# Eleven weight tiles of a two-layer mixer split into rounded part and remainder by DMAs instead of by ScalarE and VectorE

## The chip, the cores and the metric

One Trainium2 chip, and one of its cores. The metric is the time of one execution of the kernel on the device, in microseconds (us); lower is better. The engines are called PE (TensorE, matmuls), ACT (ScalarE), DVE (VectorE), POOL (GpSimd) and SP (SyncE, which here issues nearly all DMAs).

## The reference

Two layers. Each adds a mixer and then a mixture of experts to the stream `x` (256 tokens of 1024 channels, float32).

```python
h = rms_norm(x, norm_mix_g[l]) * (1.0 + sc_m) + sh_m
x = x + g_m * mixer(h, ...)
h = rms_norm(x, norm_ffn_g[l]) * (1.0 + sc_f) + sh_f
x = x + g_f * moe_ffn(h, ...)
...
proj = h @ w_in                      # in the mixer: 1024 x 7168
qa, ka, va, ub, qc, kc, vc, gates = jnp.split(proj, IN_SPLITS, axis=-1)
y_a = diff_attention(qa, ka, va) @ w_proj_a      # norm and rotary on qa, ka before
y_b = conformer_conv(ub, ...) @ w_proj_b + b_proj_b
y_c = stick_breaking(qc, kc, vc) @ w_proj_c
g = jax.nn.sigmoid(gates)            # three gates of 1024 channels
merged = g[0] * y_a + g[1] * y_b + g[2] * y_c
return merged @ w_out
```

The vectors sc_m, sh_m, g_m and so on come from `c_act @ w_mod[l]`, whose weights are read too ("mod" below). The mixture of experts has 64 experts, of which each token uses 8, and a shared one.

## The kernel before

The kernel runs, in this order: mixer of layer 0 (up to about 330 us of the profile), experts of layer 0 (to about 820), mixer of layer 1 (to about 1135), experts of layer 1 (to the end at 1628.8).

Weights come in tiles of 2 MB (128 partitions x 4096 float32), each by two DMAs of 128x2048 that SP issues (L218). The tiles stand in one list, `st`, in the order in which they are needed. Five slots of this size, `w`, take them in turn, and a load waits until the tile that was in its slot has been used. In the mixer `w_in` is 14 such tiles: qa, ka, va, uba, ubg (the two halves of ub), qc, kc, vc and six gate tiles ga0, ga1, gb0, gb1, gc0, gc1. Each tile makes four output chunks of 128 channels. The mod tiles stand between them and are summed on DVE (L530, 1024 columns at a time).

A chunk is a sum over 1024 channels in eight parts of 128. Most parts are computed in float32r (a shorter float32) with a correction. The activations stand as a rounded `hH` and a remainder `hL`, made once in `mix_norm`. The weights of each half chunk (four parts, 128x512) are split in `split`, L686 and L687:

```python
se.activation(H[:, j:], src, AF.Copy)                              # ACT: WH, rounded
ve.tensor_tensor(Lo[:, j:], src, H[:, j:].bitcast(F32), op=OP.subtract)   # DVE: WL, the remainder
```

Three matmuls then stand for each part, hH by WH, hL by WH, hH by WL (`mmj`). The other parts are computed in one plain float32 matmul of `plain` (called room in the profile) by the tile itself; the table NAT says how many of the eight. For `w_in` that is none in layer 0 and three in layer 1, so that there only the last five parts are split (WH is 128x128 and 128x512 in turn). Five pairs of WH and WL are kept (NSPLIT), made ahead of the matmuls (`ahead`).

PE's order is written by a planner: attention and convolution pieces run as generators between the half chunks (`mm_piece`), at a rate set by constants. The convolution is 31 steps on DVE for each of four channel groups (L765, room<-room,tcol,room, 128x256). The order on ACT, DVE and POOL is the scheduler's, which goes by priority and by what is ready. POOL issues none of the weight loads of the mixers.

In layer 0, after the gate tiles of C, PE comes to the tail of the attention A (lines 927 to 973): the head norms need a reciprocal root that DVE works out in eleven small steps (L455 to L464, 128x8), and PE then transposes its result (L973), before the first projection. In layer 1 the first tiles are qa (chunks up to 842 us) and va.

Of the kernel before, what the change touches and what calls it, by code (L numbers as in the profile page):

```python
# [12 lines left out]
F32R = mybir.dt.float32r  # L13
# [3 lines left out]
OP = mybir.AluOpType  # L17
# [60 lines left out]
NAT = ({"i": 0, "g": 0, "a": 4, "b": 0, "c": 4, "o": 1}, {"i": 3, "g": 3, "a": 4, "b": 0, "c": 0, "o": 3})  # L78
RAW = (1, 5)
# [89 lines left out]
def trunk(ctx, tc, A, out, dbg=None):  # L169
# [51 lines left out]

    def load_halves(src):
        t = []

        def f(k):
            if not k:
                t.append(wtile())
            sp.dma_start(t[0][:, k * 2048:(k + 1) * 2048], src[:, k * 2048:(k + 1) * 2048])
            return t[0]
        return lambda: f(0), lambda: f(1)  # L230
# [39 lines left out]
    for l in range(L):  # L270
# [9 lines left out]
        for k, s in enumerate(seq):  # L280
            if (l or k > 1) and NAT[l][{"in": "g" if s[1] in GATES else "i", "proj": s[1], "out": "o"}[s[0]]] > (4 * s[1] if s[0] == "out" else 0):
                st.held.add(len(st.items))
            if s[0] == "in" and (l or k > 1):
                st.add(("in", l, s[1]), load_tile(A["w_in"][l, s[2] // 512]))
            if s[0] == "proj":
                st.add(("proj", l, s[1]), load_tile(A["w_proj_" + s[1]][l]))
            if s[0] == "out":
                st.add(("out", l, s[1]), load_tile(A["w_out"][l, s[1]]))
            mod_at[l, s[0], s[1]] = here = [mods.pop(0) for _ in range(MOD_AT[l].count(k))]
            for m in here:  # L290
                st.add(("mod",) + m, load_mod(*m))
# [259 lines left out]

    def mix_norm(pool, l):
        i, g = NAT[l]["i"], NAT[l]["g"]
        n = min(i, g)
# [9 lines left out]
        X, XG = parts(i), parts(g)  # L564

# [30 lines left out]
    def mixer_body(l, pool, before=None):  # L596
# [27 lines left out]

        def pieces(o):
            n = plain(*o[0:2])
            return [o + (hf,) for hf in range(2) if n < (4 if o[0] == "proj" else 4 * hf + 4)]
# [13 lines left out]
        order += [p for o in seq for p in pieces(o)]  # L641
        oidx = {o: k for k, o in enumerate(order)}
        got, cur, done = {}, {}, [0]

# [4 lines left out]
        def wget(key):  # L649
            if key not in cur:  # L650
                while not loaded(key):
                    mods.extend(held)
                    held[:] = []
                    assert next(fills_[0])
                cur[key] = st.get((key[0], l, key[1]))
# [56 lines left out]
        def mm_piece(o, key, X, first, last):  # L712
            wn = weights(key) if first_split(key) else None
# [1216 lines left out]
```

## Time and profile before

| | |
|---|---|
| median of 3 runs | 1626.22 us (1619.97 to 1626.4) |
| the profiled execution's own time | 1630.43 us |
| its span in the trace | 1628.8 us |
| PE, DVE, ACT busy | 96%, 46%, 29% of the span |
| ACT L686 and DVE L687, the splits | 272 each; 147.8 and 157.2 us |
| DMA moved | 543.95 MB |

All stretches and moments below are in us from the start of the span of the profiled execution, which took 4.2 us longer than the median of the runs. A busy share of the whole span mixes four stages with different limits, so the rows further down are read by stage.

### The profile page before, as it was taken

The numbers are of one execution on the slowest core, as the hardware profiler recorded it, in microseconds if no ns is written. First come the engines' busy times: TensorE is split into PE (matmuls) and PEld (weight loads), VectorE is DVE, ScalarE is ACT, GpSimd is POOL, SyncE is SP. The second block draws the span as 40 slices with busy tenths as digits, with TensorE's granted clock in tenths as the row PEclk, the third lists the DMA queues.
The fourth block names the chain that finished last, engine by engine and source line by source line (L and its number), as shares of the span: only waits on it lengthen the run. The fifth ranks groups of instructions, "written<-read, shape, count | busy, mean of one in ns | idle before, by whom it ended". The sixth has DMA issues, their size and how long they took to land.

```text
span 1628.8 us, 25000 instructions
## 1 busy us (share of the span) xinstructions
PE 1557.7 (96%) x9710; PEld 1048.9 (64%) x9710; DVE 751.4 (46%) x1866; ACT 468.5 (29%) x911; POOL 2.9 (0%) x26
## 2 busy tenths in 40 slices
PE   6999999999999999899989999999999999998997
PEld 4999869975455454355479888798655455543543
DVE  8799989652222222122249998554422222211122
ACT  3546833421111111111144355244211111111111
POOL 0000000000000000000000000000000000000000
PEclk8999979999999999999989999899999999999999
DMA  9885418959999999999958753256599999999997
GB/s 378 354 326 225 156 53 335 387 211 384 385 419 421 419 418 419 421 420 418 417 238 335 278 214 113 99 218 272 206 381 397 421 419 419 418 419 422 419 418 283
DMA packets 76154, 543.95 MB, mean 334 GB/s; under 512 B 8576, under 2 KB 9216, under 8 KB 12544
## 3 DMA queue, kind: packets, MB, share of 16 engines
q1 hardware_dynamic: 76032, 542.31, 82.1%
q8 instruction: 78, 1.28, 0.3%
q14 instruction: 44, 0.36, 0.1%
HBM read 541.23 MB, written 1.05 MB: 333 GB/s over the span
## 4 chain that ended last, share of the span: by engine, by line
PE 71%; DMA 22%; DVE 4%; ACT 1%; issue 1%; SPq 0%; DVEq 0%; ACTq 0%
PE psA L198 32%; PE psT L198 19%; DMA w<-in_w_dram 15%; PE psS L198 12%; PE psG L198 7%; DMA wx<-in_w_dram 5%; DMA w<-in_w_mod_dram 1%; DVE w L530 1%; DVE WL L687 1%; PE psT L1675 1%; DMA xT<-in_xT_dram 0%; DVE room L765 0%; ACT h L585 0%; DMA w<-in_w_in_dram 0%; DVE nt L584 0%
## 5 line engine op out<-in xcount | busy, mean ns | idle before, releaser
L198 PE MATMUL psT<-w,xe 128*64 128x512 f32 (+2 forms) x1152 | 245.2, 606 | 6.5 <-DMA w<-in_w_dram 6.5
L198 PE MATMUL psT<-wx,xe 128*64 128x512 f32 (+2 forms) x896 | 206.9, 619 | 10.5 <-DMA wx<-in_w_dram 10.4
L198 PE MATMUL psA<-hH,WH 128*128 128x256 f32 x696 | 210.5, 302 | 1.2 <-ACT WH L686 1.2
L1659 DVE TENSOR_SCALAR oT<-psG,slot 128x256 fp32r<-128x256 f32 x54 | 26.1, 484 | 402.0 <-PE psG L198 402.0
L686 ACT ACTIVATE WH<-w 128x512 fp32r<-128x512 f32 (+2 forms) x272 | 147.8, 553 | 204.6 <-PE psA L198 184.9
L1711 DVE SCALAR_TENSOR_TENSOR Y<-psS,gt,Y 128x512 fp32r<-128x512 f32 x108 | 81.1, 751 | 264.1 <-ACT Y L1710 264.1
L198 PE MATMUL psA<-hH,WL 128*128 128x256 f32 x696 | 197.8, 284 | 1.3 <-DVE WL L687 1.3
L198 PE MATMUL psA<-hL,WH 128*128 128x256 f32 x696 | 197.5, 284 | 0.7 <-DVE hL L575 0.7
L687 DVE TENSOR_TENSOR WL<-w,WH 128x512 fp32r<-128x512 f32 (+2 forms) x272 | 157.2, 590 | 59.7 <-ACT WH L686 59.1
L198 PEld LDWEIGHTS psT<-w,xe 128*64 128x64 f32 (+2 forms) x1152 | 77.5, 130 | 140.1 <-issue 122.9
L198 PE MATMUL psA<-room,w 128*128 128x256 f32 x592 | 147.0, 393 | 1.1 <-ACT room L578 1.1
L198 PEld LDWEIGHTS psT<-wx,xe 128*64 128x64 f32 (+2 forms) x896 | 66.5, 132 | 125.4 <-issue 102.6
L1710 ACT ACTIVATE Y<-psS,gt 128x512 fp32r<-128x512 f32 x108 | 74.3, 688 | 219.3 <-PE psS L198 219.3
L198 PEld LDWEIGHTS psA<-hH,WH 128*128 128x128 f32 x696 | 133.1, 191 | 5.1 <-ACT WH L686 2.8
L198 PEld LDWEIGHTS psA<-hL,WH 128*128 128x128 f32 x696 | 133.1, 191 | 3.0 <-DVE hL L575 0.9
L198 PEld LDWEIGHTS psA<-hH,WL 128*128 128x128 f32 x696 | 132.9, 191 | 2.2 <-DVE WL L687 2.1
L1649 ACT ACTIVATE sl<-psT 128x256 f32<-128x256 f32 x54 | 20.7, 383 | 382.8 <-PE psT L198 382.8
L198 PEld LDWEIGHTS psA<-room,w 128*128 128x128 f32 x592 | 110.8, 196 | 17.8 <-issue 2.9
L198 PE MATMUL psA<-oT,Y 128*128 128x256 f32 x864 | 116.0, 286 | 0.9 <-ACT Y L1710 0.8
L530 DVE SCALAR_TENSOR_TENSOR w<-w,room 128x1024 f32<-128x1024 f32 x96 | 115.6, 1219 | 1.1 <-DMA w<-in_w_mod_dram 1.0
L198 PEld LDWEIGHTS psA<-oT,Y 128*128 128x128 f32 x864 | 105.7, 189 | 3.7 <-ACT Y L1710 3.4
L765 DVE SCALAR_TENSOR_TENSOR room<-room,tcol,room 128x256 f32<-128x256 f32 x240 | 103.9, 480 | 0.0
(586 smaller groups left out, 2102.3 us busy)
## 6 DMA issues: line engine op xcount, KB each, us to landing
w<-in_w_dram SPq DMA_DIRECT2D x200, 1024.0 KB, 19.8
wx<-in_w_dram SPq DMA_DIRECT2D x160, 1024.0 KB, 19.3
w<-in_w_in_dram SPq DMA_DIRECT2D x56, 1024.0 KB, 8.2
w<-in_w_mod_dram SPq DMA_DIRECT2D x48, 1024.0 KB, 9.1
w<-in_w_out_dram SPq DMA_DIRECT2D x8, 1024.0 KB, 8.0
wx<-in_w_dram SPq DMA_DIRECT2D x4, 2048.0 KB, 21.6
w<-in_w_dram SPq DMA_DIRECT2D x4, 2048.0 KB, 23.5
w<-in_w_proj_a_dram SPq DMA_DIRECT2D x4, 1024.0 KB, 8.0
```

The lines of the kernel that those rows point to most:

```text
L198: pe.matmul(out=o, lhsT=lhsT, rhs=rhs, start=start, stop=stop, skip_group_check=True)
L530: ve.scalar_tensor_tensor(t[:, j], t[:, j], 1.0, crow, op0=OP.mult, op1=OP.mult, accum_out=modv[l][:, c:c + 1])
L686: se.activation(H[:, j:], src, AF.Copy)
L687: ve.tensor_tensor(Lo[:, j:], src, H[:, j:].bitcast(F32), op=OP.subtract)
L765: ve.scalar_tensor_tensor(yv[:, ch], hp[:, ch, w:w + S], wc, yv[:, ch], op0=OP.mult, op1=OP.add)
L1649: se.activation(sl, b[:, 0:FF], AF.Silu)
L1659: ve.tensor_scalar(oT, bg[:, 0:S], slot[:, k_:k_ + 1], None, op0=OP.is_equal)
L1675: pe.transpose(out=b[:, j * P:(j + 1) * P], in_=hh[:, j], identity=ident)
L1710: se.activation(Y[:, hf], b, AF.Copy, scale=gt)
L1711: ve.scalar_tensor_tensor(Y[:, 2 + hf], b, gt, Y[:, hf].bitcast(F32), op0=OP.mult, op1=OP.subtract)
```

## The change

For the tiles named in CAST (five in layer 0, six in layer 1) the split is made by the DMA queue. `load_cast` loads the tile by two GpSimd DMAs of 128x2048 into a float32r view of a `w` slot: that is the rounded part. A second `w` slot ("lo") is filled in `load_rest`: ACT writes the negated rounded part, and a GpSimd DMA that adds brings the same weights from memory a second time, so that the remainder is left. Each such tile so takes two of the five slots and is read twice. `prepare_upto` starts the second part LEAD = 14 half chunks before the tile is used. The matmuls of these tiles read the slots themselves; there is no WH or WL. In layer 1 all eight parts of `h` are now split (`full`), since the cast tiles use three float32r matmuls for every part; the other tiles still use three plain parts. Counts over the program: splits 272 to 184 on ACT and on DVE each, 22 new negations on ACT, 44 DMAs on POOL, 22 fewer on SP, plain float32 matmuls 72 fewer and 216 float32r ones more, in layer 1 three more `hH` and three more `hL`.

```diff
@@ -76,6 +76,9 @@
        "uba": OFF_UB, "ubg": OFF_UB + 512}
 GATES = [f"g{b}{h}" for b in "abc" for h in range(2)]
 NAT = ({"i": 0, "g": 0, "a": 4, "b": 0, "c": 4, "o": 1}, {"i": 3, "g": 3, "a": 4, "b": 0, "c": 0, "o": 3})
+
+CAST = (("kc", "vc", "ga1", "gc1", "gb1"), ("va", "ubg", "kc", "ga1", "gb1", "gc1"))
+LEAD = 14
 RAW = (1, 5)
 NORM1 = 3
 NORM2 = 5
@@ -218,6 +221,20 @@
                 sp.dma_start(t[:, k * h:(k + 1) * h], src[:, k * h:(k + 1) * h])
             return t
         return f
+
+    def load_cast(src):
+        def f():
+            t = wtile()
+            for k in range(2):
+                ge.dma_start(t[:, k * 2048:(k + 1) * 2048].bitcast(F32R), src[:, k * 2048:(k + 1) * 2048])
+            return t
+        return f
+
+    def load_rest(hi, lo, src):
+        for k in range(2):
+            h = slice(k * 2048, (k + 1) * 2048)
+            se.activation(lo[:, h].bitcast(F32R), hi[:, h], AF.Copy, scale=-1.0)
+            ge.dma_start(lo[:, h].bitcast(F32R), src[:, h], accum_op=OP.add)
 
     def load_halves(src):
         t = []
@@ -278,6 +295,14 @@
                 seq.append(("proj", br.lower()))
         seq += [("out", 0), ("out", 1)]
         for k, s in enumerate(seq):
+            if s[0] == "in" and s[1] in CAST[l]:
+                st.held.update((len(st.items), len(st.items) + 1))
+                st.add(("in", l, s[1]), load_cast(A["w_in"][l, s[2] // 512]))
+                st.add(("lo", l, s[1]), wtile)
+                mod_at[l, s[0], s[1]] = here = [mods.pop(0) for _ in range(MOD_AT[l].count(k))]
+                for m in here:
+                    st.add(("mod",) + m, load_mod(*m))
+                continue
             if (l or k > 1) and NAT[l][{"in": "g" if s[1] in GATES else "i", "proj": s[1], "out": "o"}[s[0]]] > (4 * s[1] if s[0] == "out" else 0):
                 st.held.add(len(st.items))
             if s[0] == "in" and (l or k > 1):
@@ -549,9 +574,11 @@
     def chan_sum(b, x, w, first, last):
         mm(b[:, 0:S], w, x, start=first, stop=last)
 
+    full = []
+
     def mix_norm(pool, l):
         i, g = NAT[l]["i"], NAT[l]["g"]
-        n = min(i, g)
+        n = min(i, g) if not CAST[l] else 0
         hH, hL = (pool.tile([P, KC - n, S], F32R, name=k, tag=k) for k in ("hH", "hL"))
         half = [pool.tile([P, 4, S], F32, name="ts", tag=t) for t in ("va", "rka")]
         ts = [half[j // 4][:, j % 4] for j in range(KC)]
@@ -562,6 +589,7 @@
             return [(plain[:, j],) if j < m else (hH[:, j - n], hL[:, j - n]) for j in range(KC)]
 
         X, XG = parts(i), parts(g)
+        full[:] = parts(n)
 
         def scaled(j, r):
             ve.scalar_tensor_tensor(ts[j], xT[:, j], modA[l][:, j:j + 1], r, op0=OP.mult, op1=OP.mult)
@@ -622,7 +650,12 @@
         def plain(kind, n):
             return NAT[l]["g" if n in GATES else "i" if kind == "in" else "o" if kind == "out" else n]
 
+        def is_cast(o):
+            return o[0] == "in" and o[1] in CAST[l]
+
         def pieces(o):
+            if is_cast(o):
+                return []
             n = plain(*o[0:2])
             return [o + (hf,) for hf in range(2) if n < (4 if o[0] == "proj" else 4 * hf + 4)]
 
@@ -638,9 +671,27 @@
             else:
                 seq += [("proj", br.lower(), q) for q in range(4)]
         seq += [("out", 0, ch) for ch in range(KC)]
-        order += [p for o in seq for p in pieces(o)]
+        behind, preps, count = {}, [], 0
+        for o in seq:
+            if is_cast(o):
+                if o[2] == 0:
+                    preps.append((count - LEAD, o[1]))
+                behind.update({o + (hf,): len(order) for hf in range(2)})
+            order += pieces(o)
+            count += 2
         oidx = {o: k for k, o in enumerate(order)}
+        when = {o + (hf,): 2 * k + hf for k, o in enumerate(seq) for hf in range(2)}
         got, cur, done = {}, {}, [0]
+
+        def prepare(n):
+            load_rest(st.tiles["in", l, n], st.tiles["lo", l, n], A["w_in"][l, (OFF[n] if n in OFF else OFF_G + "abc".index(n[1]) * D + int(n[2]) * 512) // 512])
+
+        def prepare_upto(at):
+            while preps and preps[0][0] <= at:
+                st.upto(len(st.items))
+                if ("lo", l, preps[0][1]) not in st.tiles:
+                    return
+                prepare(preps.pop(0)[1])
 
         def loaded(key):
             st.upto(len(st.items))
@@ -648,10 +699,14 @@
 
         def wget(key):
             if key not in cur:
-                while not loaded(key):
+                while not loaded(key) or is_cast(key) and not loaded(("lo", key[1])):
                     mods.extend(held)
                     held[:] = []
                     assert next(fills_[0])
+                if is_cast(key):
+                    if preps and preps[0][1] == key[1]:
+                        prepare(preps.pop(0)[1])
+                    cur["lo", key[1]] = st.tiles.pop(("lo", l, key[1]))
                 cur[key] = st.get((key[0], l, key[1]))
                 mods.extend(held)
                 held[:] = mod_at.get((l,) + key, [])
@@ -710,6 +765,18 @@
             mm(o, w[1][:, j], x[0], start=False, stop=last)
 
         def mm_piece(o, key, X, first, last):
+            prepare_upto(when.get(key, -1))
+            if is_cast(key):
+                weights(key)
+                w = [cur[k, key[1]].bitcast(F32R).rearrange("p (j f) -> p j f", j=KC)[:, 4 * key[3]:4 * key[3] + 4, key[2] * P:(key[2] + 1) * P]
+                     for k in ("in", "lo")]
+                for j in range(4):
+                    mmj(o, w, j, full[4 * key[3] + j], first and j == 0, last and j == 3)
+                if key[3] and key[2] == 3:
+                    for k in ("in", "lo"):
+                        st.held.discard(st.pos[k, l, key[1]])
+                ahead(behind[key] + NSPLIT[l])
+                return
             wn = weights(key) if first_split(key) else None
             w = split_of(key) if key in oidx else None
             for j in range(4):
```

Three places in the order of the engines. On DVE in layer 0 at the tail of the attention A, the eleven steps of the reciprocal root (rsv, rst, rsy) stand, before, each with a step of the convolution (L765) between:

```order
L455 TENSOR_SCALAR rsv<-psT 128x8
L765 SCALAR_TENSOR_TENSOR room_80<-room_78,tcol_72,room_80 128x256
L457 TENSOR_SCALAR rsy<-rsv 128x8
L765 SCALAR_TENSOR_TENSOR room_80<-room_78,tcol_72,room_80 128x256
L460 TENSOR_TENSOR rst<-rsy 128x8
L765 SCALAR_TENSOR_TENSOR room_80<-room_78,tcol_72,room_80 128x256
L462 SCALAR_TENSOR_TENSOR rst<-rst,rsv 128x8
```

In the changed kernel (where the lines are 25 higher here, and the scans of attention C are L1084 and L1085):

```order
L480 TENSOR_SCALAR rsv<-psT 128x8
L482 TENSOR_SCALAR rsy<-rsv 128x8
L485 TENSOR_TENSOR rst<-rsy 128x8
L1084 SCALAR_TENSOR_TENSOR room_78<-room_78 128x128
L1084 SCALAR_TENSOR_TENSOR room_78<-room_78 128x256
L487 SCALAR_TENSOR_TENSOR rst<-rst,rsv 128x8
L1085 TENSOR_TENSOR room_78<-room_78 128x384
L489 SCALAR_TENSOR_TENSOR rsy<-rst,rsy 128x8
L1084 SCALAR_TENSOR_TENSOR room_78<-room_78 128x128
L485 TENSOR_TENSOR rst<-rsy 128x8
```

The convolution's steps have all been done by then, and scans of attention C stand in some of the places.

On ACT at the opening of layer 1's mixer, the end of the norm (hH), the splits of qa, and the two evacuations of qa's chunks (L1131 and L1133) before:

```order
L571 ACTIVATE hH<-ts,modv_162 128x256 x4
L686 ACTIVATE WH<-w 128x512 x4
L1131 ACTIVATE room_7212<-psA 128x512
L1133 ACTIVATE room_7210<-psA,tcol_73 128x512
L1131 ACTIVATE room_7212<-psA 128x512
```

and in the changed kernel, where L741 is the split and L236 the negation for va:

```order
L599 ACTIVATE hH<-ts,modv_162 128x256 x4
L741 ACTIVATE WH<-w 128x512 x4
L236 ACTIVATE w<-w 128x2048 x2
L1198 ACTIVATE room_7077<-psA 128x512
L1200 ACTIVATE room_7075<-psA,tcol_73 128x512
```

The two negations stand behind the four splits of qa, so that the adding DMAs of va are issued only after those.

On POOL in layer 0 (L229 are the casting loads, L237 the adding ones, in the order kc, vc, ga1, gc1, gb1):

```order
L229 DMA w<-in_w_in_dram 128x2048 x2
L237 DMA w<-in_w_in_dram 128x2048 x2
L229 DMA w<-in_w_in_dram 128x2048 x2
L237 DMA w<-in_w_in_dram 128x2048 x2
L229 DMA w<-in_w_in_dram 128x2048 x3
```

None of these stood on POOL before; each adding load stands ahead of the next tile's casting load, and waits on ACT.

## Rows read from the trace of the kernel before

**Rows 1.** The page, part 1: busy us, share of the span and instructions of each engine

```profile
PE 1557.7 (96%) x9710; PEld 1048.9 (64%) x9710; DVE 751.4 (46%) x1866; ACT 468.5 (29%) x911; POOL 2.9 (0%) x26
```

**Rows 2.** Windows: length, PE, PEld, DVE, ACT, POOL (count), PEclk, DMA share, GB/s

```profile
400.00:800.00 400.00, 385.05 (x2311) 196.69 (x2309) 87.69 (x203) 64.78 (x118) 0.20 (x1) 0.99 1.01 416
79.00:205.00 126.00, 126.00 (x961) 114.11 (x962) 120.76 (x277) 80.47 (x146) 0.00 (x0) 1.00 0.61 234
205.00:231.00 26.00, 22.46 (x102) 14.51 (x100) 22.39 (x63) 10.81 (x25) 0.00 (x0) 0.67 0.00 1
283.00:300.00 17.00, 15.63 (x124) 14.89 (x124) 15.35 (x29) 8.81 (x15) 0.00 (x0) 1.00 1.01 418
...
834.00:1011.00 177.00, 175.24 (x1143) 155.17 (x1142) 154.53 (x396) 81.99 (x180) 0.00 (x0) 1.00 0.59 227
...
1011.00:1032.00 21.00, 20.02 (x118) 15.38 (x117) 9.82 (x29) 7.04 (x16) 0.00 (x0) 0.86 0.27 101
```

**Rows 3.** The page, part 5, the splits: busy us, mean ns, idle before and releaser

```profile
L686 ACT ACTIVATE WH<-w 128x512 fp32r<-128x512 f32 (+2 forms) x272 | 147.8, 553 | 204.6 <-PE psA L198 184.9
...
L687 DVE TENSOR_TENSOR WL<-w,WH 128x512 fp32r<-128x512 f32 (+2 forms) x272 | 157.2, 590 | 59.7 <-ACT WH L686 59.1
```

**Rows 4.** The page, part 6: DMA issues, KB each, median us to landing

```profile
w<-in_w_dram SPq DMA_DIRECT2D x200, 1024.0 KB, 19.8
...
w<-in_w_in_dram SPq DMA_DIRECT2D x56, 1024.0 KB, 8.2
```

**Rows 5.** The chain that ended last, 79 to 210 us, longest pieces: start, length, what

```profile
97.95 5.69 PE psA L198 x48
...
111.39 5.69 PE psA L198 x48
118.09 8.73 PE psA L198 x72
```

**Rows 6.** Timeline of PE, one chunk's 24 matmuls in layer 0: start, length

```profile
98.14 0.29 PE L198 MATMUL psA<-hH,WH 128*128 128x256 f32 x1
...
100.99 0.28 PE L198 MATMUL psA<-hH,WH 128*128 128x256 f32 x1
```

**Rows 7.** Timeline of PE, one chunk of layer 1, from its plain matmuls

```profile
875.14 1.46 PE L198 MATMUL psA<-room,w 128*128 128x256 f32 x6
...
878.22 0.95 PE L198 MATMUL psS<-halves,room 128*128 128x2 f32 x8
```

**Rows 8.** Timeline of SP's queue: the issues of kc and of a mod tile

```profile
63.49 0.80 SPq L218 DMA_DIRECT2D w<-in_w_in_dram  x2
78.08 0.80 SPq L218 DMA_DIRECT2D w<-in_w_mod_dram  x2
```

**Rows 9.** Timeline of ACT in layer 0, a split before kc is used

```profile
85.40 0.64 ACT L686 ACTIVATE WH<-w 128x512 fp32r<-128x512 f32 x1 [0.79 <-PE psA L198]
```

**Rows 10.** Timeline of DVE in layer 0, the last sum of a mod tile before 106

```profile
104.18 1.21 DVE L530 SCALAR_TENSOR_TENSOR w<-w,room 128x1024 f32<-128x1024 f32 x1
```

**Rows 11.** Timeline of DVE, the reciprocal root of attention A in layer 0

```profile
213.27 0.16 DVE L455 TENSOR_SCALAR rsv<-psT 128x8 f32<-128x8 f32 x1
213.35 0.48 DVE L765 SCALAR_TENSOR_TENSOR room<-room,tcol,room 128x256 f32<-128x256 f32 x1
...
217.99 0.17 DVE L464 SCALAR_TENSOR_TENSOR rsy<-rst,rsy 128x8 f32<-128x8 f32 x1
```

**Rows 12.** Timeline of PE, what waited for it

```profile
218.31 0.59 PE L973 MATMUL psT<-ident,rsy 128*4 128x128 f32 x2 [3.24 <-DVE rsy L464]
```

**Rows 13.** Timeline of SP's queue at the opening of layer 1's mixer

```profile
810.16 28.13 SPq L218 DMA_DIRECT2D w<-in_w_in_dram  x6
```

**Rows 14.** Timeline of ACT at that opening: the last splits of qa

```profile
834.90 1.67 ACT L686 ACTIVATE WH<-w 128x512 fp32r<-128x512 f32 x3 [2.62 <-PE psA L198]
```

**Rows 15.** Timeline of PE at that opening: va's first matmuls

```profile
842.06 1.46 PE L198 MATMUL psA<-room,w 128*128 128x256 f32 x6
844.03 0.39 PE L198 MATMUL psA<-hH,WH 128*128 128x256 f32 x1 [0.51 <-ACT WH L686]
```

## The prediction

> **What bounds the kernel now.** I read the page's busy shares first, then windows by stage, then the chain of waits with timelines at the places that the change touches. Over the whole span PE is 96% busy and DVE 46% [rows 1], but that mixes stages. In the two expert stages the DMA share is 1.01 at 415 to 416 GB/s: they run at the speed of their weight stream, and the change does not touch them. A mixer that ends earlier lets the next stage start earlier, so what a mixer gains, the run gains; and what it loses, the run loses. In the mixers DMA has room (0.61 in 79 to 205, 0.59 in 834 to 1011), DVE is nearly full (120.76 of 126, 154.53 of 177), and still PE has no gap in the first of these stretches and 1.76 us of gaps in the second [rows 2]. So in most of both mixers PE is the bound, and the splits on ACT and DVE, 147.8 and 157.2 us in all [rows 3], are hidden beside it: removing 88 of 272 of each gives nothing by itself. It pays only where PE waits for DVE, and the mixers show few such places.
>
> **The change part by part**, against the profiled execution (1630.43 us; 4.2 above the median of 1626.22, from which the forecast is taken).
>
> 1. *Plain matmuls that become float32r ones, layer 1.* A chunk there takes 878.22 - 875.14 = 3.08 us [rows 7]; a fully split chunk of 24 matmuls in layer 0 has a pitch of (100.99 - 98.14)/24 = 0.119, so 2.85 us [rows 6]. Six cast tiles of four chunks: 24 x 0.23 = **-5.5 us**. This is on PE's own path, in stretches where PE is busy, so I count all of it.
>
> 2. *PE's gaps in layer 1, 834 to 1011.* 1.76 us [rows 2], among them 0.51 waiting for a split of va, which is a cast tile now [rows 15]. The six tiles take 48 of the splits from DVE and ACT: **-1.8**, between 0 and -2.6 (some matmuls also run at a longer pitch while DVE is late).
>
> 3. *Tail of attention A, layer 0.* 205 to 231 is 26 us with PE busy 22.46 at a granted clock of 0.67, the lower of the two levels in much of it [rows 2]. PE waits 3.24 us for the reciprocal root [rows 12], whose eleven small steps run from 213.27 to 218.16, because a convolution step of 0.48 that issues every 0.39 us stands behind nearly each of them [rows 11]. In the changed order those convolution steps have been done before, since DVE has 40 fewer splits in this layer. Eleven x 0.39 = **-4.3**. The bounds: 0, if the scans of attention C that now stand there take the same time, and -8, from layer 1, where the same tail with a chunk of about 3 us takes 21 [rows 2], so 18 against 26.
>
> 4. *Merging in layer 0, 283 to 300.* PE's gaps are 17 - 15.63 = 1.37 [rows 2], with DVE 90% busy: **-1.4**, bounds 0 and -1.4.
>
> 5. *The new pieces on ACT.* 22 negations of 128x2048. Four splits of 128x512 take 4 x 0.557 = 2.2 (1.67 for three, [rows 14]); one instruction of that size has one start instead of four, so I take 1.9 as an estimate. 42 us come against 88 splits that go (49): ACT is below half busy in all these windows [rows 2], so nothing.
>
> 6. *The transfers.* 22 MB more are read. By 8.2 us to landing for 1 MB with some queue and 19.8 in the full queue of the expert stages [rows 4], an adding load lands 8 to 20 us after its issue; below 8 nothing speaks. No row shows a GpSimd load of this kind, with a cast or an add. I take 8.2, because the mixers' DMA share is nearer to that of the plain `w_in` loads. What the loads must meet:
>  - kc, layer 0. The rounded part can be issued at 63.5, as now. The second slot comes free with the mod tile whose successor SP issues at 78.08 [rows 8]. The negations stand behind splits on ACT that end near 82 and at 86.04 [rows 9], so the adds go out near 84 and 88 and land at 92 and 96. kc's first chunk starts at 97.95 [rows 5], its second half 1.43 later. Margin 2 to 6 us: nothing.
>  - vc. Its second slot is kc's rounded one, free when kc ends near 110.4, just ahead of qc's stretch [rows 5]. Its rounded part is issued when a mod tile has been summed, not later than 105.4 [rows 10], and lands near 110 to 114. Negations to 112.5 and 115, adds landing near 121 and 123. qc's four chunks of 2.85 start at 110.8, and so vc at about 122.5, its second half at 123.9: nothing, up to 3 if the rounded part is late.
>  - ga1, gc1 and gb1 have over ten us more by the same counting: nothing.
>  - va, layer 1. The casting load is released with the `w_in` loads of 810 [rows 13]. The negations stand behind the splits of qa, which end at 836.57 [rows 14]: 838.5 and 840.4, the adds landing at 846.7 and 848.6. va starts at 842.06 [rows 15]. PE waits 4.6 us there, and then 0.5 for the second half (needed 1.43 after the first): **+5.1**. The evacuation of qa stands behind those negations on ACT, but needs PE's end at 842 anyway.
>  - The adds on POOL hold back the next tile's casting loads; nobody else issues there.
>
> 7. *Three more hH and hL in layer 1's opening.* Each hH takes 0.51 or so on ACT, on a path where PE waits; DVE makes the hL beside it: **+0.6**, bounds 0 and 1.5.
>
> 8. *Slots.* Two of five go to one tile, so mod tiles and later tiles load later. Cover: DVE sums mod tiles at its own pace, and DMA is idle 40% of the time. Nothing; gone if a tile lands after its first chunk.
>
> Sum: -5.5 - 1.8 - 4.3 - 1.4 + 5.1 + 0.6 = **-7.3 us**; 1626.2 - 7.3 = **1619**. Its own range, from the bounds of terms 2, 3 and 7 and a share of 6: 1612 to 1627.
>
> **The rivals.**
>
> *A. The loads land late, and it is slower.* The place: the three tightest tiles. For an adding load that lands L after its issue, PE waits L - 11.4 for kc (88 to 99.4), L - 8.9 for vc (115 to 123.9, both shifted alike) and L - 3.1 for va (840.4 to 843.5). With L = 19.8 [rows 4] that is 8.4 + 10.9 + 16.7 = 36.0; less the gains of 13.0, plus 0.6, +23.6, so 1650. It decides from 3L - 23.4 = 12.4, that is L = 11.9; by over 8 us slower from 14.6. A cause could be a load issued by POOL that waits for DVE, which is 96% busy between 79 and 205 [rows 2]. For it: DVE never rests there. Against it: the sums and remainders on DVE are operations of two inputs, and POOL did nothing in the mixers before, so no row shows either. Chance 0.20.
>
> The page "SBUF — State Buffer" of the Trainium skill (the warning ahead of the section "A bandwidth-pool intuition that's wrong (but worth ruling out)") says that a DMA issued from GpSimd cannot have its descriptors written while VectorE is in a 2-port performance mode; on that rule such loads would be late here, as in A. The same page, section "Who interferes with whom", finds that `tensor_tensor` did not stall such DMAs, which would leave the sum as it is. No trace of the kernel before can show which holds.
>
> *B. The tails do not gain.* The scans of attention C and the mod sums take the places of the convolution steps, and the merge waits for ACT instead. Terms 3 and 4 go: -5.5 - 1.8 + 5.1 + 0.6 = -1.6, so 1625. For it: in the changed order scans do stand between the steps of the root, and PE ran the tail at the lower clock, with 22.46 of 26 busy. Chance 0.17.
>
> *C. A larger gain.* The casting load and the negation of va come ahead of qa's last splits, or the add lands in 4 us, so that PE never waits, and the tail of A takes 18 us as in layer 1: -5.5 - 1.8 - 8 - 1.4 + 0.6 = -16.1, so 1610. For it: 1 MB at the expert stages' 415 GB/s [rows 2] is 2.5 us, so a load into an idle queue can be that short, and the DMA share is low at 840. Against it: the order on ACT. Chance 0.23.
>
> **How the numbers follow.** A measurement of this kernel can tell about 0.5% from no change, 8 us, so from 1618.1 to 1634.4 is no change. The forecast has 0.40; its middle lies at the edge of that band, so 0.22 of it is faster and 0.18 no change. C (0.23) is faster. B (0.17) is no change but for 0.02 slower. A (0.20) is slower but for 0.03, where L lies between 11.9 and 14.6. Faster 0.45, same 0.36, slower 0.19. The range takes in C with the larger bound of term 2 and 3 us more for fewer late splits (1606), and A up to L = 17.5, 3 x 17.5 - 23.4 - 12.4 = +16.7 (1643). Outside it are the rest of A, some 0.09, and 0.08 of larger gains than C.
>
> **What would show it.** The profile after should have w_in loads on a GpSimd queue with a landing time near 8 us (A: over 12); chunks of cast tiles in layer 1 of 2.85 us; a wait of PE for a DMA of 4 to 5 us at va in layer 1 and none at kc and vc of layer 0 (A: at all three; C: none); the reciprocal root of layer 0's tail in about half its 4.9 us, with PE's wait of 3.24 gone (B: still there). The expert stages should last as long as before. It would be wrong if the expert stages change, if PE waits at tiles that were not split by the queue because their slot came free late, or if the plain loads' landing grows well beyond 8 us.

## The result and the profile after

The change makes the kernel slower: median 1685.06 us (1682.98 to 1688.72, 4 runs) against 1625.41 of the kernel before, ratio 1.0352 with a 95% interval of 1.0325 to 1.0379. That is 59.7 us more, outside the forecast's range (1606 to 1643) and of the other sign.

Busy shares (the page, part 1), the matmuls of the cast tiles and the splits on DVE (part 5):

```profile
PE 1579.0 (94%) x9782; PEld 1067.2 (63%) x9782; DVE 712.2 (42%) x1781; ACT 466.4 (28%) x852; POOL 34.4 (2%) x70
...
L201 PE MATMUL psA<-hH,w 128*128 128x256 f32 x704 | 143.7, 300 | 33.8 <-DMA w<-in_w_in_dram 33.7
...
L742 DVE TENSOR_TENSOR WL<-w,WH 128x512 fp32r<-128x512 f32 (+2 forms) x184 | 105.2, 594 | 73.9 <-ACT WH L741 73.5
```

The splits went as the diff says [rows 3]: 39 us less busy on DVE. But PE, whose cast chunks take less time at the same clock than the chunks that they replace in layer 1, is busy 21 us longer than before [rows 1], and 33.7 us of its new idle time is spent waiting for loads of w_in, of which there was none. Where in the run is that? One place is common to all runs: the router's 16 matmuls after each mixer, in the chain that ended last (start, length). Before:

```profile
342.13 3.46 PE psS L198 x16
...
1147.68 3.46 PE psS L198 x16
```

and after:

```profile
365.15 3.46 PE psS L201 x16
...
1205.80 3.46 PE psS L201 x16
```

So layer 0's mixer ends 23.0 us later, and from one router to the next it is 840.65 instead of 805.55, 35.1 more. That is the mixer of layer 1, for its first matmuls come 23.0 later too (849.76 against 826.72), so the experts of layer 0 between took as long as before. From there to the end it is 481.3 us against 481.1: the expert stages did not change, as forecast. Both mixers lose.

The transfers (part 6: KB, median us to landing) and the queue of POOL (part 3: packets, MB, share of 16 engines):

```profile
w<-in_w_mod_dram SPq DMA_DIRECT2D x48, 1024.0 KB, 13.6
w<-in_w_in_dram POOLq DMA_DIRECT2D x44, 1024.0 KB, 11.1
w<-in_w_in_dram SPq DMA_DIRECT2D x34, 1024.0 KB, 13.5
```
```profile
q0 software_dynamic: 6336, 46.14, 10.5%
```

The loads of w_in land later than the 8.2 us before [rows 4], the plain ones too, and so do the mod tiles (9.1 on the page of before); those of w_out and of the projections do not. For the adding loads alone (line 237), issue to landing:

```profile
DMA to landing us min/median/max: 8.0/11.3/18.8
```

Two of the places where PE waits, in the timeline of PE: vc in layer 0 and va in layer 1. The waits stand in brackets, one for each half of the tile.

```profile
132.95 0.51 PE L201 MATMUL psA<-hH,w 128*128 128x256 f32 x2 [2.87 <-DMA w<-in_w_in_dram]
140.39 0.80 PE L201 MATMUL psA<-hH,w 128*128 128x256 f32 x2 [5.74 <-DMA w<-in_w_in_dram]
...
873.91 0.79 PE L201 MATMUL psA<-hH,w 128*128 128x256 f32 x2 [8.09 <-DMA w<-in_w_in_dram]
879.77 0.79 PE L201 MATMUL psA<-hH,w 128*128 128x256 f32 x2 [2.93 <-DMA w<-in_w_in_dram]
```

The loads that they wait for, in POOL's timeline: vc's second adding load went out at 121.56 and landed 18.8 us later; va's went out at 862.06 and 863.85, which is the forecast's 838.5 and 840.4 plus the 23 that layer 0 was late, and landed after 11.8 and 15.9 instead of 8.2.

```profile
121.56 0.86 POOL L237 DMA_DIRECT2D w<-in_w_in_dram  x1 [1.40 <-ACT w L236]
...
862.06 0.88 POOL L237 DMA_DIRECT2D w<-in_w_in_dram  x1 [33.99 <-ACT w L236]
863.85 0.86 POOL L237 DMA_DIRECT2D w<-in_w_in_dram  x1 [0.91 <-ACT w L236]
```

Behind such a wait PE does not go on at its former speed. Windows around va (length, PE, PEld, DVE, ACT, POOL, PEclk, DMA share, GB/s):

```profile
870.00:875.00 5.00, 1.09 (x5) 1.10 (x6) 1.70 (x4) 1.55 (x4) 0.00 (x0) 0.50 1.02 210
875.00:880.00 5.00, 2.07 (x10) 1.77 (x10) 0.00 (x0) 0.00 (x0) 0.00 (x0) 0.50 0.62 128
880.00:885.00 5.00, 5.00 (x27) 4.37 (x28) 0.00 (x0) 0.60 (x1) 0.00 (x0) 0.74 0.00 0
885.00:890.00 5.00, 5.00 (x40) 4.52 (x39) 1.36 (x5) 1.19 (x2) 0.00 (x0) 1.00 0.00 0
```

The granted clock is at the lower of the two levels from 870 on (it read 1.00 up to 868, while PE had been waiting since 865.8). It is back at the upper one within the window from 880 to 885: in windows of 1 us it reads 0.50 up to 882 and 1.00 from 883. In these 5 us 27 matmuls are recorded, and 40 in the next. The same rows show what the queue does: with the DMA engines full (1.02) they moved 210 GB/s, half of the 416 that a full share gave in the expert stages [rows 2].

### The profile page after: what moved, and what is told of

Same layout as the page of the kernel before. It is cut to its first block, busy times and chain, and to the rows that moved or that the text cites. A ratio compares the mean times of both kernels' runs of the same rounds, so it can differ in the third digit from the quotient of the medians.

```text
span 1687.1 us, 24939 instructions
## 1 busy us (share of the span) xinstructions
PE 1579.0 (94%) x9782; PEld 1067.2 (63%) x9782; DVE 712.2 (42%) x1781; ACT 466.4 (28%) x852; POOL 34.4 (2%) x70
## 3 DMA queue, kind: packets, MB, share of 16 engines
q0 software_dynamic: 6336, 46.14, 10.5%
## 4 chain that ended last, share of the span: by engine, by line
PE 56%; DMA 33%; DVE 6%; issue 3%; ACT 2%; SPq 0%; POOL 0%; DVEq 0%; ACTq 0%; POOLq 0%
PE psA L201 23%; PE psT L201 16%; DMA w<-in_w_dram 14%; PE psS L201 10%; DMA wx<-in_w_dram 10%; DMA w<-in_w_in_dram 7%; PE psG L201 6%; DMA w<-in_w_mod_dram 3%; DVE w L555 2%; DVE room L832 1%; PE psT L1742 0%; DVE WL L742 0%; ACT w L236 0%; PE psG L1002 0%; ACT h L613 0%
## 5 line engine op out<-in xcount | busy, mean ns | idle before, releaser
L201 PE MATMUL psT<-wx,xe 128*64 128x512 f32 (+2 forms) x896 | 204.8, 608 | 11.8 <-DMA wx<-in_w_dram 11.8
L201 PE MATMUL psA<-hH,w 128*128 128x256 f32 x704 | 143.7, 300 | 33.8 <-DMA w<-in_w_in_dram 33.7
L201 PEld LDWEIGHTS psA<-hH,w 128*128 128x128 f32 x704 | 117.9, 202 | 37.7 <-DMA w<-in_w_in_dram 35.7
L742 DVE TENSOR_TENSOR WL<-w,WH 128x512 fp32r<-128x512 f32 (+2 forms) x184 | 105.2, 594 | 73.9 <-ACT WH L741 73.5
L741 ACT ACTIVATE WH<-w 128x512 fp32r<-128x512 f32 (+2 forms) x184 | 96.7, 553 | 134.0 <-PE psA L201 86.8
L201 PE MATMUL psA<-hH,WH 128*128 128x256 f32 x416 | 126.4, 304 | 0.0
L1716 ACT ACTIVATE sl<-psT 128x256 f32<-128x256 f32 x54 | 20.7, 383 | 379.6 <-PE psT L201 379.6
L555 DVE SCALAR_TENSOR_TENSOR w<-w,room 128x1024 f32<-128x1024 f32 x96 | 114.9, 1219 | 21.1 <-DMA w<-in_w_mod_dram 21.0
L201 PE MATMUL psA<-hH,WL 128*128 128x256 f32 x416 | 119.3, 287 | 4.7 <-DVE WL L742 4.7
L201 PE MATMUL psA<-hL,WH 128*128 128x256 f32 x416 | 118.9, 286 | 0.0
L201 PE MATMUL psA<-room,w 128*128 128x256 f32 x448 | 115.4, 406 | 1.9 <-ACT room L606 1.9
L201 PE MATMUL psA<-hL,w 128*128 128x256 f32 x352 | 102.9, 292 | 0.0
L201 PEld LDWEIGHTS psA<-room,w 128*128 128x128 f32 x448 | 87.5, 204 | 15.7 <-ACT room L606 2.2
## 6 DMA issues: line engine op xcount, KB each, us to landing
w<-in_w_dram SPq DMA_DIRECT2D x200, 1024.0 KB, 19.8
w<-in_w_in_dram POOLq DMA_DIRECT2D x44, 1024.0 KB, 11.1
w<-in_w_in_dram SPq DMA_DIRECT2D x34, 1024.0 KB, 13.5
w<-in_w_dram SPq DMA_DIRECT2D x4, 2048.0 KB, 23.9
```

Of the source, the lines that this page charges most:

```text
L201: pe.matmul(out=o, lhsT=lhsT, rhs=rhs, start=start, stop=stop, skip_group_check=True)
L555: ve.scalar_tensor_tensor(t[:, j], t[:, j], 1.0, crow, op0=OP.mult, op1=OP.mult, accum_out=modv[l][:, c:c + 1])
L1716: se.activation(sl, b[:, 0:FF], AF.Silu)
```

## The experiments

The theory after this view: the adding loads are dear, and PE waits for them (theory 1). Rivals: the two slots that each tile takes starve other tiles (2); any load from POOL is late (3). Kernels that leave out part of the computation have other values in the experts' router; only in one run, named below, did that change the experts' work. So beside the medians the table gives the two marks of the profile: router of layer 0, and router to router, each against the kernel before (342.13 and 805.55). Ratios are to runs of the kernel before on the same chip.

| run | median us | ratio (95%) | layer 0 | layer 1 |
|---|---|---|---|---|
| the change | 1685.1 | 1.0352 (1.0325 to 1.0379) | +23.0 | +35.1 |
| e1 no adding loads | 1627.1 | 0.9987 (0.9963 to 1.0011) | -2.7 | -0.4 |
| e2 second casting load | 1648.2 | 1.0117 (1.0072 to 1.0161) | -1.5 | +19.2 |
| e3 five loose tiles | 1633.0 | 1.0017 (0.9991 to 1.0043) | -4.6 | +3.5 |
| e4 layer 1 only | 1659.6 | 1.0178 (1.0132 to 1.0225) | -1.2 | +32.1 |
| e6 without va | 1663.3 | 1.0233 (1.0204 to 1.0263) | +14.8 | +14.4 |
| e7 LEAD 28 | 1683.3 | 1.0350 (1.0322 to 1.0377) | +20.9 | +31.6 |
| e8 two tiles of layer 0 | 1628.5 | 1.0016 (0.9996 to 1.0036) | -2.3 | -2.9 |
| e10 by columns | 1708.3 | 1.0490 (1.0462 to 1.0519) | +32.8 | +46.7 |
| e11 adding loads not waited for | 1667.2 | 1.0234 (1.0191 to 1.0278) | +17.1 | +20.4 |
| e12 as e1, negation on POOL | 1681.5 | 1.0323 (1.0280 to 1.0366) | +23.6 | +28.0 |
| e13 casting loads alone | 1622.9 | 0.9968 (0.9948 to 0.9989) | -2.4 | -6.5 |
| e14 as e3, negation on POOL | 1659.6 | 1.0199 (1.0168 to 1.0230) | +13.7 | +17.8 |
| e15 a quarter added | 1673.7 | 1.0274 (1.0243 to 1.0305) | -1.2 | +9.8 |
| e16 second reading alone | 1629.8 | 1.0009 (0.9989 to 1.0029) | +2.2 | -3.4 |
| e17 adding alone | 1646.4 | 1.0115 (1.0086 to 1.0143) | +8.8 | +4.3 |

A mark comes from one profile, and that of the kernel before was itself 4.2 us above the median. The same code of layer 0 gave +23.0 in the change and +14.8 in e6, and where a layer is as in the kernel before the marks read -1.2 (layer 0 of e4) and -2.9 (layer 1 of e8). So a few us in either column say nothing.

**e1, the adding loads left out.**

```diff
-            ge.dma_start(lo[:, h].bitcast(F32R), src[:, h], accum_op=OP.add)
```

> The adding loads are left out (the second slot holds only the negated rounded part, so the remainder is missing from the result); casting loads, negations, slots and matmuls stay. Theory 1, the adding loads are what is slow (they landed 8.0 to 18.8 us after their issue, and PE waited 33.7 us for them): PE's waits for w_in go, the granted clock comes back, and the time is near the sum without its waits, 1612 to 1625. Theory 2, the two slots of five that each such tile takes make mod tiles and later tiles late: the waits for slots stay, 1650 or more. Theory 3, any load issued by GpSimd is late whatever it does: casting loads still land after 11 us and part of the loss stays, 1630 to 1650.

The time is that of the kernel before: 58 us of the loss hang on the adding loads, and casting loads, negations and slots without them cost nothing net. Theories 2 and 3 fall. But it is not below before either, so the forecast's gains are not seen in the total; see e13.

**e2, a second casting load instead.**

```diff
-            ge.dma_start(lo[:, h].bitcast(F32R), src[:, h], accum_op=OP.add)
+            ge.dma_start(lo[:, h].bitcast(F32R), src[:, h])
```

> The adding load becomes a second casting load of the same bytes, at the same place behind the same negation, on the same queue (the second slot then holds the rounded part again, so the remainder is wrong). Theory 1 in its narrow form, it is the addition that is slow: the loads land in about 8 us and the time falls to 1615 to 1635. Theory 1 in its wide form, it is the second reading with its traffic that is slow, with or without addition: 1660 or more. Theories 2 and 3: unchanged, 1675 to 1690.

Between the two forms of theory 1: the second reading behind the negation costs 21 us over e1, and the addition 37 more. At line 237 of this kernel, where the second casting load stands in the adding load's place:

```profile
DMA to landing us min/median/max: 5.1/5.8/11.3
```

Same bytes, same place, same queue: the median is half as long without the addition. PE's wait at va, whose two loads landed there after 9.1 and 9.7 us, is 5.34 us, where the forecast had 5.1 by a plain load's 8.2:

```profile
848.15 0.79 PE L201 MATMUL psA<-hH,w 128*128 128x256 f32 x2 [5.34 <-DMA w<-in_w_in_dram]
```

**e3, e4, e6, e8: which tiles.** Only the table CAST is edited, for instance in e3:

```diff
-CAST = (("kc", "vc", "ga1", "gc1", "gb1"), ("va", "ubg", "kc", "ga1", "gb1", "gc1"))
+CAST = (("gc1", "gb1"), ("ga1", "gb1", "gc1"))
```

> Only the five tiles for which PE did not wait in the profile after stay with the queue: gc1 and gb1 in layer 0, ga1, gb1 and gc1 in layer 1. Theory 1: no tile is late any more; the sum has 12 of 24 chunks at 0.23 us (-2.8), part of the tails, and the opening of layer 1 is as before: 1617 to 1628. Theory 2: each tile costs its share of slots, 5/11 of 59 us: about 1650. Theory 3: lateness without a waiting PE costs nothing, as theory 1.

> Layer 0 as before the change, layer 1 as after it. In the profile after, the router of layer 0 comes 23 us later than before and the one of layer 1 another 35. If the two layers' losses stand by themselves (theory 1): 1655 to 1665. If layer 1's loss is partly what layer 0 left behind (slots and queues out of step, theory 2): under 1645.

> va of layer 1 is split by the engines again, the other ten tiles as in the change. PE waited 8.09 and 2.93 us for va's adding loads, and PE was 14.2 us later behind va than in the run without adding loads. Theory 1 (waits add up tile by tile, each with a stretch at the lower clock behind it): 1669 to 1674. If the queue is merely saturated, the wait moves on to ubg and kc: 1680 or more.

> Only gc1 and gb1 of layer 0 stay with the queue, layer 1 as before the change. In the run with five loose tiles, layer 0 ended 4.6 us earlier than before and layer 1 took 3.5 longer. Theory A (layer 0's tail gains from less work on DVE, and layer 1 gives back at its opening and its tail): 1620 to 1624, below the kernel before by 3 to 6 us. Theory B (the 4.6 is the scatter of one profile): as the kernel before, within 1.5 us.

Five tiles with time to spare cost nothing that can be told (e3), but they bring no gain either: 1633.0, where 1617 to 1628 was expected. So nearly all of the loss comes from the six tight ones. Layer 1 alone costs +32 with layer 0 at its old time: the layers' losses stand by themselves. Without va the median is 22 us lower, and by the marks 20.7 in layer 1, more than its two waits of 11.0 and more than was expected. (The 8.2 less in layer 0, where the code is the same, are scatter.) Two tiles of layer 0 gain nothing that can be told (e8, and theory B there).

**e7, LEAD = 28, and e10, cut by columns.**

```diff
-LEAD = 14
+LEAD = 28
```
```diff
+        H, Lo, W = (t.rearrange("p (j f) -> p j f", j=8) for t in (hi, lo, src))
...
+            h = slice(k * 256, (k + 1) * 256)
+            se.activation(Lo[:, :, h].bitcast(F32R), H[:, :, h], AF.Copy, scale=-1.0)
+            ge.dma_start(Lo[:, :, h].bitcast(F32R), W[:, :, h], accum_op=OP.add)
```

> LEAD 28 instead of 14: the second part may be prepared 14 half chunks earlier, some 20 us. Theory 1a (the adding loads are only issued too late): the waits for kc of both layers, ubg and ga1 go, and the time falls to 1655 to 1668. Theory 1b (their issue is set by slots and by the casting load and the negation that stand ahead of them, not by LEAD): 1678 to 1690.

> The second part is cut by output columns instead of by input rows: each of the two adding loads brings the columns of two chunks (pieces of 1 KB instead of 8 KB), so that a tile's first chunk needs only the first of them. Theory 1 (PE waits for the landing of the second adding load, 2.9 to 5.7 us at each late tile): 1660 to 1672. If shorter pieces make adding loads slower still: 1685 or more.

Neither mends it. The adding loads went out at nearly the same times with LEAD 28 (vc's at 117.91 and 120.19, in the change at 119.28 and 121.56): the slot, the casting load and the negation set them. Pieces of 1 KB made it 23 us worse. POOL's queue took 12.3% of the span there instead of 10.5, and PE's waits for w_in were 37.2 us in all, so that cutting by columns did not take them away; where the rest of the 23 us lies was not followed up.

**e13, the casting loads alone: what there was to gain.** The second slot, the negation and the adding load are taken out.

```diff
-                     for k in ("in", "lo")]
+                     for k in ("in", "in")]
...
-                st.add(("lo", l, s[1]), wtile)
...
-            prepare_upto(when.get(key, -1))
```

> Casting loads alone: no second slot, no negation, no adding load; the matmuls read the rounded part twice (the remainder is missing). This is the bound of what the change could give if the remainder cost nothing. Theory of the forecast's gains (5.5 + 1.8 + 4.3 + 1.4): 1612 to 1617. If those gains were not there to be had: 1622 to 1628.

Ratio 0.9968 (0.9948 to 0.9989): with a remainder that costs nothing the change would be worth about 5 us, 2 to 8, not 13. By the marks layer 1 gave 6.5 (the forecast had 7.3 there before its costs) and layer 0 2.4 of 5.7, both with their scatter of some 3 us. e1 shows in ACT's timeline what a negation can do to layer 1:

```profile
865.70 1.91 ACT L236 ACTIVATE w<-w 128x2048 fp32r<-128x2048 f32 x1 [4.05 <-DMA w<-in_w_in_dram]
867.51 0.29 ACT L740 ACTIVATE WH<-w 128x128 fp32r<-128x128 f32 x1
867.71 0.58 ACT L1197 ACTIVATE room<-psA 128x512 f32<-128x512 f32 x1
```

ubg's negation held ACT for 4.05 us until its casting load had landed, with a split and the evacuation L1197 in line behind it, and PE waited 1.87 us for that evacuation. What the negations cost in all is not shown: e1 lies 4 us above e13, the intervals overlap, and e1 takes the second slots as well.

**e11, the adding loads not waited for, and e12 and e14, the negation on POOL.**

```diff
-                     for k in ("in", "lo")]
+                     for k in ("in", "in")]
```
```diff
-            se.activation(lo[:, h].bitcast(F32R), hi[:, h], AF.Copy, scale=-1.0)
+            ge.tensor_scalar(lo[:, h].bitcast(F32R), hi[:, h], -1.0, None, op0=OP.mult)
```

> All transfers of the change run, adding loads too, but the matmuls read the rounded part in place of the remainder, so that PE never waits for an adding load (the remainder's product is wrong). Without adding loads the time was that of before, with them 59 us more. Theory W (it is PE's wait for their landing, with the slow clock behind it): 1628 to 1640. Theory T (their traffic, which holds the 16 DMA engines twice as long per byte, delays the plain loads and mod tiles): 1655 or more. In between, both, in that proportion.

> As the run without adding loads, and the negations are made by POOL instead of ACT. In that run the mixer of layer 1 gained nothing: the negation of ubg stood 4.05 us on ACT waiting for its casting load, with a split and an evacuation behind it, and two negations of 1.9 us stood in the tail of attention A. Theory N (the negations on ACT, in order, eat the gain): 1617 to 1623. Theory O (the tails' length is set by something else): 1625 to 1629.

> The five loose tiles, complete, with the negation on POOL. Theory N: layer 1 no longer gives back, 1617 to 1623, below the kernel before. Theory O: as the five loose tiles before, 1626 to 1630.

In e11 18 us of the 58 go with PE's own wait; 40 stay, as in theory T. There PE waits for splits and evacuations on ACT instead (7.6 us for WH, 7.8 for L1007), and ACT itself waits for loads: at the splits for the plain tiles, at the negations for the casting loads. In e11, and at the splits in e1 (line, in total, times, longest):

```profile
ACT WH L741 <- DMA w<-in_w_in_dram: 36.7, 9, 12.3
ACT w L236 <- DMA w<-in_w_in_dram: 31.4, 7, 10.7
```
```profile
ACT WH L740 <- DMA w<-in_w_in_dram: 4.3, 3, 2.5
```

In the change these waits are 36.1 and 23.9, in e1 4.3 and 6.7. So the adding loads also make the other loads of the mixers come late to ACT. Not all of that costs time: e16, below, has 21.3 at the splits and the time of the kernel before.

e12 and e14 were meant to free ACT, and met a new cost. POOL's negation in e12, durations in ns (min, median, max), and beside the first two DVE's splits:

```profile
L236 POOL TENSOR_SCALAR w<-w x22: 5355/5418/6325, 77.7 to 1072.6; 128x2048 fp32r<-128x2048 f32 x22
```
```profile
77.53 10.59 DVE L741 TENSOR_TENSOR WL<-w,WH 128x512 fp32r<-128x512 f32 x6
```

5.4 us where ACT takes 1.9, and six remainders on DVE took 10.59 us while POOL ran (the longest 4.13), where one takes 0.69. DVE's busy time rose from 710.5 (e1) to 777.0. So neither theory N nor O was tested by them.

**e15 to e17: bytes, or a chain of fixed delays?** e15 adds a quarter of each half; e16 and e17 clear the second slot on POOL and fill it by a casting or an adding load that nobody waits for, with no negation.

```diff
+            q = slice(k * 2048, k * 2048 + 512)
+            ge.dma_start(lo[:, q].bitcast(F32R), src[:, q], accum_op=OP.add)
```
```diff
-            se.activation(lo[:, h].bitcast(F32R), hi[:, h], AF.Copy, scale=-1.0)
+            ge.memset(lo[:, h], 0.0)
```

> Each adding load brings a quarter of its bytes (128x512 of 128x2048; the rest of the second slot keeps the negated rounded part, so the remainder is missing there); number, place and order of all instructions stay. If it is the bytes that are added (the DMA engines' time): about a quarter of the 58 us between without and with adding loads, 1636 to 1648. If it is a fixed delay of each adding load (issue, completion) on the chain from casting load over negation to PE: 1660 or more.

> The second slot is cleared by POOL and filled by a second casting load, with no negation on ACT, and the matmuls read the rounded part twice: the second reading as traffic and as a slot, with nobody waiting for it. Against the run with the casting loads alone (0.997 of before): if traffic and slots matter, 1640 or more; if only waits and ACT's order did in the run with the second casting load, 1620 to 1630.

> The same with an adding load in place of the second casting load: adding traffic with nobody waiting for it and no negation on ACT (the remainder is not formed). In the run where adding loads were not waited for the time was 1667, but there negations that wait for casting loads still stood on ACT ahead of splits. Theory T (the traffic itself): 1655 or more. Theory W (ACT and PE in line behind it): 1625 to 1640, and close to the run before it in this series.

e15's 1673.7 would speak for a fixed delay, and misleads. In this run the values differed enough for the experts of layer 1 to take their overflow path, which no other kernel here ran; it shows among PE's waits (line, in total, times, longest):

```profile
PE psG L201 <- DVE tmp L1845: 9.0, 1, 9.0
```

and its last stage, from the router on, is 516.3 us long, 35 more than in the others. By the marks the two mixers lost 8.6 us against before, so 11.7 against e1, where the whole adding load lost 61.2: 19% for a quarter of the bytes. The loss goes mostly with the bytes that are added. In POOL's queue, e16 and then e17:

```profile
q0 software_dynamic: 6336, 46.14, 7.5%
```
```profile
q0 software_dynamic: 6336, 46.14, 10.7%
```

7.5% of 1628.6 is 122 us of all 16 engines, 10.7% of 1644.4 is 176, with the same bytes. In e13, with the 22 casting loads alone, the share was 3.8% of 1620.6, 62 us. So a casting load holds the engines 2.8 us and an adding load (176 - 62)/22 = 5.2. With PE never waiting for it the addition costs 17 us (e17 over e16), which lies between the two theories of e17. Second readings and slots alone (e16) stay within 1620 to 1630, the forecast for the case that traffic and slots by themselves don't matter.

## Why the prediction was wrong

**What fell: term 6.** It took an adding load at a plain load's 8.2 us to landing "because the mixers' DMA share is nearer to that of the plain w_in loads". Measured: 8.0 at the least, 11.3 in the median, up to 18.8; the addition nearly doubles the time that a load holds the DMA engines (5.2 us against 2.8), and these were already 0.61 busy in layer 0's mixer [rows 2]. The places, the order and the moments of issue were right to within 1 us at kc and va, and at va with a load that does not add (e2) so was the wait. At vc the links ahead were too short as well: the casting loads went out at 106.58, 1.2 us after the forecast's 105.4, and landed after 10.4 and 12.2 us, so that the adds went out at 119.28 and 121.56 instead of 112.5 and 115. The bounds were in the text: 19.8 as the far end was nearer for vc than the value taken. So was the sign of being wrong: the plain loads' landing did grow well beyond 8 us, to 13.5.

**Rival A was the right case at 0.20, its price too low.** It gave 1650 at L = 19.8. At its three tiles its formula was near: the later loads of kc, vc and va landed after 14.1, 18.8 and 15.9 us, for which it gives 2.7 + 9.9 + 12.8 = 25.4, and PE waited 2.57, 8.61 and 11.02, in all 22.2. But PE also waited at ga1 of layer 0 (2.51) and at ubg (3.26) and kc (5.69) of layer 1, which the forecast held to have "over ten us more" or did not look at. And A counted waits alone. Of the loss of 58 us over e1, 33.7 us of PE's waits for w_in are seen directly. The rest is seen only in part: in matmuls at the lower clock after a wait (va: 11.0 us of wait, 14.1 us later in the sequence of PE's work, which is the same in e1), in ACT's line, where splits and negations wait 36.1 and 23.9 us for loads, and on DVE, which waits 21.0 us for mod tiles instead of 6.1 in e1. How much each has is not settled: e11 takes away PE's waits alone and keeps 40 us, e17 keeps the traffic alone and 17, but the order on ACT differs between them. DVE as the cause of late loads, which A offered, is not needed for the adding loads: in e2 loads from the same queue, at the same places and with DVE as busy (711.0 us against 712.2), landed after 5.1 us at the least and 5.8 in the median. Why the casting loads ahead of them took 8.3 (e13) to 11.1 us (the change) in the median was not separated.

**Term by term, without the adding loads.** Term 1 (-5.5): a cast chunk of layer 1 takes 2.84 us (1018.03 to 1020.87 in the timeline of PE), 2.85 was forecast. That is right; with term 2 the forecast has 7.3, and the 6.5 of e13 agrees within its scatter. Term 3 (-4.3): PE's wait of 3.24 us [rows 12] is gone, but in the profile after the root runs from 234.96 to 240.21, 5.2 us instead of 4.9 [rows 11], with scans between its steps, and the tail is hardly shorter than before:

```profile
234.96 0.17 DVE L480 TENSOR_SCALAR rsv<-psT 128x8 f32<-128x8 f32 x1 [4.38 <-PE psT L201]
...
240.04 0.17 DVE L489 SCALAR_TENSOR_TENSOR rsy<-rst,rsy 128x8 f32<-128x8 f32 x1
```
```profile
228.00:254.00 26.00, 25.11 (x98) 16.59 (x98) 12.61 (x36) 16.05 (x30) 2.30 (x3) 0.62 0.86 246
```

In 26 us PE is now busy 25.11 at a clock of 0.62, against 22.46 at 0.67 [rows 2]: the time that DVE gave back PE spent at the lower clock. That is rival B's case for this term, in this run. It does not hold in all of them. From the sums of squares for the root (psT<-ones,nsq) to the first projection (psA<-room,w) it is 21.4 us before, 20.5 in the change and 20.4 in e13, but 18.2 in e1 and 15.5 in e2 (214.12 to 229.62), with the same tiles cast in layer 0. In e2 the granted clock was back at the upper level while the tail still ran, which in the change it was not (0.50 from 249 to 253):

```profile
216.00:220.00 4.00, 3.12 (x13) 1.83 (x12) 3.79 (x15) 1.03 (x3) 0.00 (x0) 0.70 1.05 416
220.00:224.00 4.00, 4.00 (x16) 2.25 (x16) 1.84 (x7) 3.37 (x6) 0.53 (x1) 0.50 0.27 53
224.00:228.00 4.00, 4.00 (x19) 2.79 (x18) 1.13 (x3) 3.55 (x6) 0.53 (x1) 0.95 0.60 227
```

In e16, again with the same tiles, it is 21.1. So the tail gained between 0.3 and 5.9 us over these runs, and DVE's steps alone do not say how much; where it goes with the clock was looked at in e2 and the change only. Term 4 (-1.4): in the 17 us that lie as far ahead of the router as 283 to 300 did, PE's gaps are 0.96 in the change, 1.64 in e1 and 0.56 in e13, against 1.37. It gave less than forecast. Term 5 ("nothing"): the size was right (1.91 us each); but a negation that waits for a load stands ahead of other work on ACT, which the term did not price and no run shows in the total. Term 7 (+0.6): PE's wait at the opening is 1.91 instead of 1.12, so 0.8. Term 8 (slots): e16, with both slots taken, both readings and POOL's clears, stands at 1.0009, 6.9 us over e13; so these do cost, little.

## What to carry to other kernels

Moving an elementwise step into the DMA queue moves it to a resource that the kernel may be short of: price an adding load by the time that it holds the DMA engines (here nearly twice a casting load's), and by where it ends in a chain of load, negation and load, not by a plain load's landing. Give it tiles with time to spare: five such tiles cost nothing that could be told here, and gained nothing either; the six tight ones cost 57 us. When an experiment leaves part of the result out, look in the profile whether later stages still do the same work before reading its total.

## What the runs showed of the hardware that was not expected

- An adding load of 1 MB held the 16 DMA engines 5.2 us, a casting load 2.8; landing at the least 8.0 against 5.1.
- A 128x2048 multiplication on POOL took 5.4 us (ACT 1.9), and VectorE's subtractions of two SBUF operands slowed beside it, six in 10.59 us. POOL's clears of the same size in e16 (1.8 us) left DVE's busy time at 715.7 us. The Trainium skill's page "SBUF — State Buffer", section "Who interferes with whom", says that a VectorE instruction with two SBUF inputs contends with a GpSimd instruction that reads SBUF; this run agrees.
- Around PE's waits at va, of 8.09 us up to 873.91 and 2.93 up to 879.77, the granted clock read 1.00 up to 868, 0.50 from 870 to 882 and 1.00 from 883. PE had no gap from 879.77 to 890.
